# Reordering the seven products of a down projection, with fewer weight loads and the residual loaded by halves

## The chip, the cores and the metric

One core of one Trainium2 chip runs the whole kernel. The metric is device time in microseconds (us). The matmul engine is called PE below, the vector engine DVE, the scalar engine ACT, GpSimd POOL, and the queue that issues most transfers SP.

## The reference

The program is one decoder block on 1024 tokens of width 1024, with 16 meta tokens put ahead of them, all in float32. The part that matters here is the feed-forward layer, which is computed twice, before and after the token mixing:

```python
def _swiglu(x, w_gu, w_down):
    gate, up = jnp.split(x @ w_gu, 2, axis=-1)
    return (jax.nn.silu(gate) * up) @ w_down

h = h + 0.5 * _swiglu(_rmsnorm(h, ffn1_norm[l]), ffn1_w_gu[l], ffn1_w_down[l])
u = _rmsnorm(h, mix_norm[l])
...                                    # mixing: gated delta rule and RWKV-7, added to h
h = h + 0.5 * _swiglu(_rmsnorm(h, ffn2_norm[l]), ffn2_w_gu[l], ffn2_w_down[l])
return _rmsnorm(h, final_norm)[:, N_META:]
```

The hidden width is 2816. The first feed-forward layer works on 1040 columns (tokens and meta tokens), the second on 1024.

## The kernel before

Activations lie transposed, with channels on the 128 partitions and tokens along the free axis. Every float32 matrix product is made of three float32r matmuls: both operands are split into a high part (a copy on ACT into float32r, line 164) and a low part (the difference, on DVE, line 165), and high x high, high x low and low x high are added up in PSUM.

Each feed-forward product is a Strassen-Winograd product over 2 x 2 blocks, so it takes seven block products in place of eight. For the down projection (function `down`, matmuls at line 700) the left blocks are the weights W00, W01, W10, W11 (rows are halves of the 1024 outputs, columns are halves of the 2816 hidden channels), or sums of them. The right blocks are seven *forms* of the hidden activations (`FORMS`): the plain blocks b11, b21, b22, and the differences t1 to t4. Tokens are halved too: n is 520 columns in the first layer and 512 in the second. `ADDS` says to which of the four quadrants of the residual h each product is added (line 706; 0 and 1 are the two token halves of the upper 512 outputs, 2 and 3 those of the lower).

One form is one *round*, called r0 to r6 below in the order of `FORMS`. A round has four output tiles m (`HK` = 4) of 128 rows, and each has 11 blocks of 128 hidden channels, in two weight chunks of 6 and 5 (`CHUNKS`). With three matmuls per block that makes 132 matmuls of 512 columns per round in the second layer, and 264 of 256 or 264 columns in the first, where a row of 520 does not go through one matmul.

The work around each round:

- *Weights.* `weight_order` lists all chunks in the order of their use. `fetchw` loads the next one into a buffer `wraw` (two buffers) from SP's queue, and `down_weights` makes of it what the round needs. In the rounds on sums, POOL adds or subtracts it into a tile `wsum`, which holds one sum per chunk and lasts from round to round. Then the chunk, or its sum, is split into a weight tile (two tiles `w` and a third one, `w3`). `loadw` keeps the fetches two chunks ahead of the one in use.
- *Forms.* The gate and up phase stores its finished forms to device memory (line 530, SP's queue). `Hidden.load` brings those of the next round back in the course of a round (line 670, ACT's queue), and `Hidden.split` splits them in place. `Hidden.arrange` gives the places; while one round reads one set of 11, the other set is loaded.
- *Residual.* In r0 the loop loads the rows of h for output tiles m and m + 4 ahead of tile m's matmuls (lines 780 and 883, SP's queue).
- *The last two rounds of the first layer* go by columns: `down_rounds` yields r5 and r6 for the columns from 256, and then both again for the first 256, so that the norm that follows can start on the later columns. Their weights are fetched twice. Squares for the norm (line 326), the store of h (line 813), and, in the second pass, the normalised input of the mixing (line 825, split at lines 164 and 165) are put behind each output tile by `after`.
- In the second layer, `after` runs the final norm of the second token half behind r4, and that of the first half at the end.

The order of r0 to r6 is b11, t1, t2, b22, t3, b21, t4. The weights they need are W00; W10 + W11; W10 + W11 - W00; W01 less that; W00 - W10; W01; W11. An entry into `wsum` that is not a sum of the last content and one block starts from two loads: r1 loads W10 and W11, r4 loads W00 and W10.

The program is traced in this order, and a planner orders the instructions on each engine's queue by its own estimate of when they are ready; `issue_after` puts an instruction behind a given one on its queue. Each queue is executed in its order.

Of the kernel before, what the change touches and what calls it, by code (L numbers as in the profile page):

```python
# [8 lines left out]
F32 = mybir.dt.float32  # L9
# [36 lines left out]
FORMS = ("b11", "t1", "t2", "b22", "t3", "b21", "t4")  # L46
ADDS = ((0, 1, 2, 3), (1, 3), (1, 2, 3), (1,), (2, 3), (0,), (2,))
NSLOT = 28
LAST = len(FORMS) - 2
# [146 lines left out]
def down_rounds(by_columns):  # L196

    for r in range(LAST):
        yield r, None
    for cols in ((256, T // 2 - 256), (0, 256)) if by_columns else (None,):  # L200
        for r in range(LAST, len(FORMS)):
            yield r, cols


def weight_order():

    def down_order(n):
        for r, _ in down_rounds(n == 1):
            for m in range(HK):
                for k0, kk in CHUNKS:  # L210
                    yield f"wdn{n}", (r, m, k0), kk

    def tiles(cts, j=0):
        for ct in cts:
            yield "win", (ct + j % NJ,), KD

    yield from down_order(1)
    for act, it in schedule():
        yield from tiles(USES.get(act, ()), 0 if act == "segment" else it)
    for _ in range(2):  # L220
        for m in range(KD):
            yield "wout", (m,), KD

    yield None
    yield from down_order(2)


def down_weights(g, name, raw, r, m, k0, kk):

    blk = lambda i, j: g.a[name][m + HK * i][:, HF * j + k0 : HF * j + k0 + kk]  # L230
    dma = g.nc.sync.dma_start
    sums = g.nc.gpsimd.tensor_tensor
    g.wdma = dma(raw, blk(*((0, 0), (1, 1), (0, 0), (0, 1), (1, 0), (0, 1), (1, 1))[r]))
    if r in (0, LAST, LAST + 1):
        return raw
    s = g.wsum[:, m, k0 : k0 + kk]

    def other(i, j):
        with g.tc.issue_after(g.wdma.ins):
            dma(s, blk(i, j))  # L240

    if r == 1:
        other(1, 0)
        sums(s, s, raw, op=ALU.add)
    elif r == 2:
        sums(s, s, raw, op=ALU.subtract)
    elif r == 3:
        sums(s, raw, s, op=ALU.subtract)
    else:
        other(0, 0)  # L250
        sums(s, s, raw, op=ALU.subtract)
# [3 lines left out]
def fetchw(g):  # L255
# [4 lines left out]
    raw = g.wp.tile([P, KD, P], F32, name="wraw", tag="wraw", bufs=2)[:, :kk]  # L260
    if name.startswith("wdn"):
        src = down_weights(g, name, raw, *idx, kk)
    else:
        src = raw
        g.nc.sync.dma_start(raw, g.a[name][idx])
    third = False
    if name.startswith("wdn"):
        g.wcount += 1
        third = g.wcount % 3 == 0
    if third:  # L270
# [7 lines left out]
def loadw(g, name, *idx):  # L278

    while g.wfetched < len(g.worder) and g.worder[g.wfetched]:  # L280
        if g.wfetched > g.wused + AHEAD + g.worder[g.wfetched][0].startswith("wdn"):
            break
# [204 lines left out]
def gate_up(g, which, n, w, b):  # L487
# [93 lines left out]
    for i, (p, gu) in enumerate(units):  # L581
# [34 lines left out]
        else:  # L616
            mul(c21, g21, p, "b21")
            sub(g21, c21, g22, p, "t4")
# [5 lines left out]
class Hidden:  # L624
# [14 lines left out]
    def ahead(self):  # L639
        self.g.wcount = 0  # L640
# [16 lines left out]
        self.split(HF)  # L657
        yield

    def arrange(self, spare, last):  # L660
        e, o = self.even, self.odd
        self.slots = e[:HF] + (o[:HF] + e[:HF]) * 2 + o[HF:] + [spare] + o[:HF] + last

    def load(self, upto, done):
        while len(self.loads) < min(upto, len(self.slots)):
# [4 lines left out]
            self.g.nc.scalar.dma_start(t[:, 1, :].bitcast(F32), self.g.frm[rp][:, : self.n])  # L670
            self.loads.append((rp, t))

    def split(self, upto):
        while len(self.at) < min(upto, len(self.order)):
# [9 lines left out]
def down(g, hs, which, n, hidden, hooks):  # L684

    nc = g.nc
    for r, cols in down_rounds(which == 1):
        for m in range(HK):
            hidden.step(r, m)
            if r == 0:  # L690
                hooks.residual(m)
            pd = mm_tile(g, "pd", n)
            parts = [cols] if cols else halves(n)
            for k0, kk in CHUNKS:
                wd = loadw(g, f"wdn{which}", r, m, k0)
                for c0, cn in parts:
                    for k in range(k0, k0 + kk):
                        x = hidden.at[r, k]
                        for i, (u, v) in enumerate(((0, 0), (0, 1), (1, 0))):
                            nc.tensor.matmul(pd[:, c0 : c0 + cn], lhsT=wd[:, u, k - k0, :], rhs=x[:, v, c0 : c0 + cn],  # L700
                                             start=k + i == 0, stop=k == HF - 1 and i == 2)
            c0, cn = cols or (0, n)
            for o in ADDS[r]:
                t0 = o % 2 * n + c0
                hv = hs[m + o // 2 * HK][:, t0 : t0 + cn]
                nc.vector.scalar_tensor_tensor(hv, pd[:, c0 : c0 + cn], 0.5, hv, op0=ALU.mult, op1=ALU.add)
            hooks.after(r, cols, m)
# [19 lines left out]
def ffn1(g):  # L727
    tc, nc = g.tc, g.nc
    n = T // 2
    with ExitStack() as ctx:  # L730
# [38 lines left out]
        hs = {k: sp.tile([P, T], F32, name=f"h{k}") for k in (3, 7, 2, 0, 4, 1, 5, 6)}  # L769
        sum_tile = lambda shape, dtype: sp.tile(shape, dtype, name="wsum", tag="wsum", bufs=1)  # L770
        g.wsum = sum_tile([P, HK, HF, P], F32)
        spare = sp.tile([P, 2, ROW(n)], F32R, name="form")[:, :, :n]
# [4 lines left out]
        def residual(m):  # L777
            for k in (m, m + HK):
                with tc.issue_after(g.wdma.ins):
                    nc.sync.dma_start(hs[k], g.a["hT"][k])  # L780

        hooks.residual = residual

        def before_last():
            early.close()
            t = sum_tile([P, 5, 2, ROW(n)], F32R)
            hidden.slots += [t[:, i, :, :n] for i in range(5)]
            g.upctx = ExitStack()
# [12 lines left out]
            hooks.todo = []  # L801

        def after(r, cols, m):
# [4 lines left out]
            s = 0 if cols[0] else 1  # L808
            k = m + HK * (r - LAST)
            t0, sn, _ = SEGS[s]  # L810
            rms = hooks.rms[s]
            rms.add(hs[k][:, t0 : t0 + sn])
            nc.sync.dma_start(g.hdr[s][k], hs[k][:, t0 : t0 + sn])
            if k == KD - 1:
                rs = g.un.tile([P, 528], F32, name="nrs", tag="nrs", bufs=2)
                rms.finish(rs)
# [3 lines left out]
                else:  # L820
                    nc.sync.dma_start(g.rdr, rs[:, :sn])
            if s == 1:
                k, rs = hooks.todo.pop(0)
                t = g.un.tile([P, 528], F32, name="nt", tag="nt", bufs=2)
                nc.vector.scalar_tensor_tensor(t, hs[k][:, SEGS[0][0] :], g.V("gm", k), rs, op0=ALU.mult, op1=ALU.mult)
                g.u.append(u_tile(g, t))

# [5 lines left out]
def ffn2(g):  # L833
# [3 lines left out]
    with ExitStack() as ctx:  # L837
# [34 lines left out]
        hs = {k: sp.tile([P, SEQ], F32, name=f"hh{k}") for k in (3, 7, 2, 0, 4, 1, 5, 6)}  # L872
        g.wsum = sp.tile([P, HK, HF, P], F32, name="wsum", tag="wsum", bufs=1)
        hidden.odd = hidden.places("t3", "22", "t4", "t1")
        e = hidden.even
        hidden.arrange(e[HF], e[4:9])
        hooks = K()

        def residual(m):
            for k in (m, m + HK):  # L880
                for s, h in enumerate((g.h2dr, g.h3dr)):
                    with tc.issue_after(g.wdma.ins):
                        nc.sync.dma_start(hs[k][:, s * n : (s + 1) * n], h[k])

        hooks.residual = residual

        def final_tiles(s):
# [6 lines left out]
            hooks.rs, hooks.rows = rows[3], rows[4:]  # L894
# [3 lines left out]
        def after(r, cols, m):  # L898
            s, k = int(r < LAST), m + HK * (r - LAST)
            blk = lambda k: hs[k][:, s * n : (s + 1) * n]  # L900
            if k < 0 and k + 1:
                return
            if s or k == 0:
                hooks.sum = final_tiles(s)
            for i in range(KD - 1) if s else [k] * (k < KD - 1):
                hooks.sum.add(blk(i))
            if not s and k < KD - 1:
                return
            rs = hooks.rs
            hooks.sum.finish(rs, blk(KD - 1))  # L910
            for k in range(KD):
                o = hooks.rows[k % len(hooks.rows)]
# [949 lines left out]
```

## Time and profile before

| | |
|---|---|
| median of 3 runs | 3060.49 us (3057.82 to 3062.16) |
| profiled execution | 3060.95 us, of which 3058.4 us are the span of the trace |
| mean granted TensorE clock | 0.986 |
| PE busy | 2909.5 us, 95% of the span |
| DVE, ACT, POOL busy | 2181.6, 1448.8, 481.8 us |
| r0 to r6 of the first layer | 474.1 to 742.0 us |
| mixing | from 742 us to the second layer |
| r0 to r6 of the second layer | 2805.1 to 3044 us |

A busy PE in the table counts a matmul as busy until its modelled end, and the ends of pipelined matmuls overlap, so the number of matmuls in a stretch says more on its pace than the busy time. The stretches of the rounds are found by counting the matmuls of line 700.

### The profile page before, as it was taken

How to read it: one execution, taken by the hardware profiler on the slowest of the kernel's cores; microseconds unless marked ns; L12 is line 12 of the kernel's file. 1: busy time of each engine (PE TensorE's matmuls, PEld its weight loads, DVE VectorE, ACT ScalarE, POOL GpSimd, SP SyncE). 2: the span in 40 equal slices, each digit the busy share in tenths (PEclk: the TensorE clock that was granted, in tenths of full speed). 3: DMA queues.
4: the chain of work that ended last, by engine and by line, in shares of the span. 5: the costliest groups of instructions: out<-in, count | busy, mean ns of one | idle time of the engine just before them, and what ended most of it. 6: DMA issues, size and time to landing. Idle time of an engine off the chain costs nothing.

```text
span 3058.4 us, 62929 instructions
## 1 busy us (share of the span) xinstructions
PE 2909.5 (95%) x25630; PEld 2510.0 (82%) x25630; DVE 2181.6 (71%) x4103; ACT 1448.8 (47%) x2562; POOL 481.8 (16%) x550
## 2 busy tenths in 40 slices
PE   8999999998999999999998999999999999999898
PEld 8999999997877888888776777777777788887676
DVE  6566667756668777788877887777866766667774
ACT  5222233334646556565566556655644432223343
POOL 0333221512000000000000100000000033331520
PEclk9999999999999999999999999999999999999999
DMA  3233338665222323333232332233354233336753
GB/s 121 94 105 105 105 122 290 193 193 157 84 69 69 76 69 75 77 86 83 86 96 71 79 82 76 77 83 85 103 150 164 77 104 104 104 104 235 240 185 119
DMA packets 295489, 351.51 MB, mean 115 GB/s; under 512 B 173392, under 2 KB 179536, under 8 KB 295200
## 3 DMA queue, kind: packets, MB, share of 16 engines
q1 hardware_dynamic: 271216, 303.44, 33.1%
q10 hardware_dynamic: 23904, 43.86, 4.4%
q8 instruction: 201, 3.29, 0.5%
q14 instruction: 88, 0.72, 0.1%
q0 software_dynamic: 80, 0.19, 0.0%
HBM read 279.50 MB, written 67.91 MB: 114 GB/s over the span
## 4 chain that ended last, share of the span: by engine, by line
PE 48%; DVE 10%; ACT 6%; DMA 3%; issue 2%; POOL 1%; SPq 0%; ACTq 0%; DVEq 0%; POOLq 0%
PE pp L313 16%; PE pg L500 12%; PE pd L700 3%; PE pwo L313 3%; DVE w L165 2%; ACT w L164 1%; PE pg L524 1%; DVE tb L1524 1%; DVE Xb L1526 1%; PE cs L1156 1%; PE vp L1209 1%; DMA wsum<-in_wdn 1%; PE mp L1209 1%; DMA wraw<-in_wdn 1%; DVE mt L1632 1%
## 5 line engine op out<-in xcount | busy, mean ns | idle before, releaser
L313 PE MATMUL pp<-uk,w 128*128 128x512 f32 (+2 forms) x4824 | 967.7, 346 | 13.0 <-DVE w L165 8.1
L313 PEld LDWEIGHTS pp<-uk,w 128*128 128x128 f32 x4824 | 741.5, 190 | 110.2 <-DVE w L165 15.8
L700 PE MATMUL pd<-form,w 128*128 128x256 f32 (+2 forms) x2652 | 444.7, 328 | 43.4 <-DVE w L165 22.3
L165 DVE TENSOR_TENSOR w<-wraw,w 128x1024 fp32r<-128x1024 f32 (+2 forms) x314 | 390.5, 1245 | 122.0 <-ACT w L164 118.8
L700 PEld LDWEIGHTS pd<-form,w 128*128 128x128 f32 x2652 | 393.3, 194 | 93.9 <-DVE w L165 32.3
L164 ACT ACTIVATE w<-wraw 128x1024 fp32r<-128x1024 f32 (+2 forms) x314 | 314.5, 1002 | 269.4 <-PE pg L500 119.7
L500 PE MATMUL pg<-bt,w 128*128 128x256 f32 (+2 forms) x2520 | 400.8, 317 | 0.3 <-DVE w L165 0.3
L500 PEld LDWEIGHTS pg<-bt,w 128*128 128x128 f32 x2520 | 360.2, 188 | 33.4 <-DVE w L165 0.7
L506 DVE TENSOR_TENSOR c<-c,pg 128x520 f32<-128x520 f32 (+1 forms) x280 | 189.3, 688 | 233.0 <-PE pg L500 208.6
L500 PE MATMUL pg<-b,w 128*128 128x256 f32 (+2 forms) x2160 | 347.8, 317 | 0.0
L500 PEld LDWEIGHTS pg<-b,w 128*128 128x128 f32 x2160 | 309.8, 188 | 28.0
L164 ACT ACTIVATE w<-wrx 128x1024 fp32r<-128x1024 f32 (+1 forms) x64 | 58.3, 912 | 282.1 <-PE pg L500 239.6
L470 POOL TENSOR_TENSOR wrx<-wrx 128x512 f32<-128x512 f32 x38 | 52.5, 1383 | 726.0 <-DVE w22b L165 547.8
L164 ACT ACTIVATE w<-wsum 128x768 fp32r<-128x768 f32 x64 | 50.3, 788 | 173.7 <-PE pd L700 58.9
L1526 DVE TENSOR_TENSOR Xb<-Xb,tb 115x126 f32<-115x126 f32 (+22 forms) x496 | 125.1, 252 | 8.8
L1524 DVE TENSOR_TENSOR tb<-Ub,Xb 115x126 f32<-115x126 f32 (+22 forms) x496 | 123.7, 249 | 9.3 <-DMA Ub<-scr 2.2
L1333 DVE SCALAR_TENSOR_TENSOR acc<-xr,pk,acc 128x528 f32<-128x528 f32 (+1 forms) x144 | 108.8, 756 | 28.9 <-ACT acc L1329 28.3
L165 DVE TENSOR_TENSOR form<-form 128x512 fp32r<-128x512 f32 (+1 forms) x149 | 123.1, 871 | 7.5 <-ACT form L164 7.5
L165 DVE TENSOR_TENSOR w<-wsum,w 128x768 fp32r<-128x768 f32 x64 | 75.6, 1187 | 64.3 <-ACT w L164 64.3
L164 ACT ACTIVATE form<-form 128x512 fp32r<-128x512 f32 (+1 forms) x149 | 84.6, 623 | 42.5 <-DMA form<-frm 31.6
L313 PE MATMUL pwo<-uk,w 128*128 128x512 f32 x384 | 99.3, 411 | 4.1 <-DVE w L165 1.9
L313 PEld LDWEIGHTS pwo<-uk,w 128*128 128x128 f32 x384 | 73.4, 196 | 21.6 <-ACT w L164 2.3
(426 smaller groups left out, 4438.6 us busy)
## 6 DMA issues: line engine op xcount, KB each, us to landing
wraw<-in_win SPq DMA_DIRECT2D x150, 512.0 KB
wraw<-in_wdn SPq DMA_DIRECT2D x64, 384.0 KB
wraw<-in_wgu SPq DMA_DIRECT2D x44, 512.0 KB
wrx<-in_wgu SPq DMA_DIRECT2D x44, 512.0 KB
wraw<-in_wdn SPq DMA_DIRECT2D x64, 320.0 KB
frm<-c SPq DMA_DIRECT2D x77, 260.0 KB
frm<-c SPq DMA_DIRECT2D x77, 256.0 KB
form<-frm ACTq DMA_DIRECT2D x77, 256.0 KB
```

The lines of the kernel that those rows point to most:

```text
L164: g.nc.scalar.activation(hi, src, AF.Copy)
L165: (eng or g.nc.vector).tensor_tensor(lo, src, hi.bitcast(F32), op=ALU.subtract)
L313: g.nc.tensor.matmul(ps, lhsT=l, rhs=r, start=i == 0, stop=i == n - 1)
L470: sums.tensor_tensor(a22, a21, a22, op=ALU.add)
L500: nc.tensor.matmul(ps[:, c0 : c0 + cn], lhsT=l[:, x, k, :], rhs=r[:, k, y, c0 : c0 + cn], start=i == 0, stop=i == 3 * HK - 1)
L506: nc.vector.tensor_tensor(o, x, y, op=ALU.add)
L524: nc.tensor.matmul(ps[:, c0 : c0 + cn], lhsT=l[:, x, k, :], rhs=r[:, k, y, c0 : c0 + cn], start=i == 0, stop=i == 6 * HK - 1)
L700: nc.tensor.matmul(pd[:, c0 : c0 + cn], lhsT=wd[:, u, k - k0, :], rhs=x[:, v, c0 : c0 + cn], start=k + i == 0, stop=k == HF - 1 and i == 2)
L1209: g.nc.tensor.matmul(ps[e][HS[dst], c0 : c0 + CB], lhsT=l, rhs=r, start=True, stop=True)
L1333: nc.vector.scalar_tensor_tensor(acc[:, :n], xr[:, tap : tap + n], V("convw", ct * 4 + tap), acc[:, :n], op0=ALU.mult, op1=ALU.add)
L1524: nc.vector.tensor_tensor(tv, U[:, i, i + 1 :].unsqueeze(2).to_broadcast([npt, nt, ncc]), X[:, i, 0:ncc].unsqueeze(1).to_broadcast([npt, n ...
L1526: nc.vector.tensor_tensor(X[:, i + 1 :, 0:ncc], X[:, i + 1 :, 0:ncc], tv, op=ALU.add)
```

## The change

- `FORMS` becomes t4, t1, t2, b22, b11, t3, b21, so the weights of r0 to r6 are W11; W10 + W11; W10 + W11 - W00; W01 less that; W00; W00 - W10; W01. From one to the next sum only one block is new. In r0 and in r4 a block is loaded straight into `wsum` and split from there, without `wraw` (tile 0 of r0 is still loaded through `wraw`, and again into `wsum` for r1). The number of chunk loads goes from 88 to 58 in the first layer and from 72 to 58 in the second. POOL still has 32 sums per layer.
- `ADDS` follows. t4 goes to one quadrant, so r0 needs only the first token half of the lower rows. The residual is loaded by token halves: 12 of 16 halves in the course of r0, and the first halves of the upper rows in r3, before b11 adds to all four quadrants in r4.
- The form of block 10 of t4, the last result of the gate and up phase, is not stored and loaded but split directly (`Hidden.direct`).
- Only the last round, b21, goes by columns in the first layer. Its eight weight chunks are kept for the second pass: six of them in the places of the forms t3 and 22, which are free once r5 has ended. In the second pass the first two weights of the mixing are fetched, after its output tiles 0 and 1. Their fetch within `loadw` is held off until then.
- b21 adds to the upper rows alone, so the squares and the stores of the lower rows (tiles 4 to 7, both token segments) are put between r5 and r6, and in the second pass two tiles of the mixing's input follow each output tile instead of one.
- In the second layer the final norm of the second token half stands behind r5, with the first squares of the other half.
- `wsum` is placed ahead of five of the residual's eight tiles in memory.

```diff
-FORMS = ("b11", "t1", "t2", "b22", "t3", "b21", "t4")
-ADDS = ((0, 1, 2, 3), (1, 3), (1, 2, 3), (1,), (2, 3), (0,), (2,))
-LAST = len(FORMS) - 2
+FORMS = ("t4", "t1", "t2", "b22", "b11", "t3", "b21")
+ADDS = ((2,), (1, 3), (1, 2, 3), (1,), (0, 1, 2, 3), (2, 3), (0,))
+LAST = len(FORMS) - 1
...
 def down_weights(g, name, raw, r, m, k0, kk):
     blk = lambda i, j: g.a[name][m + HK * i][:, HF * j + k0 : HF * j + k0 + kk]
+    def dma(t, i, j):
+        with ExitStack() as behind:
+            if g.wdma and t is not raw:
+                behind.enter_context(g.tc.issue_after(g.wdma.ins))
+            ins = g.nc.sync.dma_start(t, blk(i, j))
+        if t is raw:
+            g.wdma = ins
+
+    if r == LAST or (r == 0 and m == 0):
+        dma(raw, *((0, 1) if r else (1, 1)))
         return raw
     s = g.wsum[:, m, k0 : k0 + kk]
+    if r in (0, 4):
+        dma(s, r == 0, r == 0)
+        return s
+    if r == 1 and m == 0:
+        dma(s, 1, 1)
+    dma(raw, *((1, 0), (0, 0), (0, 1), None, (1, 0))[r - 1])
+    x, y = (raw, s) if r == 3 else (s, raw)
+    g.nc.gpsimd.tensor_tensor(s, x, y, op=ALU.add if r == 1 else ALU.subtract)
     return s
...
+    if down and idx[0] == LAST and g.held:
+        w = g.held.pop(0)
+    elif down and g.wcount % 3 == 0:
         w = g.wthird.tile([P, 2, CHUNKS[0][1], P], F32R, name="w3", tag="w3", bufs=1)
...
+            if p < HF - 1:
+                sub(g21, c21, g22, p, "t4")
+            else:
+                nc.vector.tensor_tensor(g21, c21, g22, op=ALU.subtract)
+                g.direct(g21)
...
+    def direct(self, src):
+        rp, t = self.loads[HF - 1]
+        split(self.g, src, t[:, 0, :], t[:, 1, :])
+        self.at[rp] = t
...
+    for r in range(len(FORMS)):
+        cols = halves(n)
+        kept = {}
         for m in range(HK):
             hidden.step(r, m)
+            hooks.before(r, m)
+
+            def w(k0):
+                kept[m, k0] = loadw(g, f"wdn{which}", r, m, k0)
+                return kept[m, k0]
+
+            product(r, m, (w, w), cols[-1:] if r == LAST else cols)
+            hooks.after(r, m, 0)
+        if r == LAST and len(cols) > 1:
+            for m in range(HK):
+                w = lambda k0: kept[m, k0]
+                product(r, m, (w, w), cols[:1])
+                if m < 2:
+                    fetchw(g)
+                hooks.after(r, m, 1)
+
+
+def residuals(r, m, load):
+
+    if r == 0:
+        if m == 0:
+            load(HK, 0)
+        if m + 1 < HK:
+            load(HK + m + 1, 0)
+        load(m, 1)
+        load(m + HK, 1)
+    if r == 3:
+        load(m, 0)
...
         def before_last():
             early.close()
             t = sum_tile([P, 5, 2, ROW(n)], F32R)
             hidden.slots += [t[:, i, :, :n] for i in range(5)]
+            hidden.load(len(hidden.slots), LAST)
+            for x in ("t3", "22"):
+                t = pools[x].tile([P, 3, 2, CHUNKS[0][1], P], F32R, name="w", tag=f"b{x}", bufs=1)
+                g.held += [t[:, i] for i in range(3)]
...
+            for s in range(2):
+                for k in range(HK, KD):
+                    squares(s, k)
```

177 lines of the change are left out of this document (79 added, 98 removed).

## The prediction, made before the change was run

> **What bounds the kernel now.** I read the page's first part (busy times), then counted the matmuls of line 700 to find the seven rounds of each layer, and then asked each round for its waits, its transfers and its engines in order of time.
>
> ```profile
> span 3058.4 us, 62929 instructions
> PE 2909.5 (95%) x25630; PEld 2510.0 (82%) x25630; DVE 2181.6 (71%) x4103; ACT 1448.8 (47%) x2562; POOL 481.8 (16%) x550
> ```
>
> PE is the bound of the whole, so only stretches in which it starves can give time. The stretches of r0 to r4 of the first layer, and of r5 with r6 in two column passes, with line 700 alone (stretch, length, PE busy and matmuls, weight loads, granted clock, DMA share, GB/s):
>
> ```profile
> 474.10:513.20 39.10, 34.20 (x264) 33.72 (x265) 0.91 0.93 328
> 513.20:550.20 37.00, 33.87 (x266) 33.28 (x265) 0.95 0.74 245
> 550.20:589.90 39.70, 35.20 (x266) 34.49 (x265) 0.91 0.60 183
> 589.90:621.40 31.50, 31.50 (x266) 31.50 (x265) 1.00 0.65 221
> 621.40:655.10 33.70, 32.24 (x267) 31.80 (x266) 1.00 0.58 177
> 655.10:697.90 42.80, 38.14 (x288) 35.19 (x287) 1.00 0.68 189
> 697.90:742.00 44.10, 35.16 (x243) 32.86 (x243) 0.92 0.60 172
> ```
>
> The fourth row is a round without a gap: 266 matmuls in 31.5 us, 0.1184 us each, so 264 need 31.3 us. Against that the rows lose 7.8, 5.7, 8.4, 0.2 and 2.4 us, and the two column passes, 528 matmuls or 62.5 us in 86.9 us, lose 24.4: 48.9 us in all. The second layer, r0 to r6:
>
> ```profile
> 2805.10:2839.90 34.80, 31.24 (x132) 24.33 (x132) 1.00 1.01 363
> 2839.90:2881.10 41.20, 33.55 (x128) 25.89 (x129) 0.92 0.75 243
> 2881.10:2914.90 33.80, 31.94 (x132) 25.46 (x131) 0.95 0.60 188
> 2914.90:2946.20 31.30, 31.30 (x139) 25.91 (x138) 1.00 0.70 235
> 2946.20:2980.40 34.20, 31.02 (x134) 24.58 (x133) 1.00 0.45 143
> 2980.40:3013.60 33.20, 30.76 (x134) 24.66 (x133) 1.00 0.53 170
> 3013.60:3044.00 30.40, 30.01 (x133) 24.52 (x131) 1.00 0.20 56
> ```
>
> Here 139 matmuls take 31.3 us, so 132 need 29.7; the losses are 5.1, 11.5, 4.1, 1.6, 4.5, 3.5 and 0.7, together 31.0 us. Both layers lose 79.9 us, and that is all the change can win in them.
>
> Why they lose it. In r0 the DMA engines are full: the transfers from 470 to 512 us are
>
> ```profile
> DMA packets 5932, 13.93 MB, mean 332 GB/s; under 512 B 671, under 2 KB 671, under 8 KB 5928
> ...
> form<-frm ACTq DMA_DIRECT2D x17, 260.0 KB
> h<-in_hT SPq DMA_DIRECT2D x8, 520.0 KB
> frm<-c SPq DMA_DIRECT2D x6, 260.0 KB
> ...
> wsum<-in_wdn SPq DMA_DIRECT2D x2, 384.0 KB
> wsum<-in_wdn SPq DMA_DIRECT2D x1, 320.0 KB
> ```
>
> and a weight chunk behind the residual comes late. In r1 and r2 ACT's splits wait for the sums, which begin from two loads in r1 (474 to 590 us; waits in total, times, longest):
>
> ```profile
> ACT w L164 <- POOL wsum L244: 15.2, 5, 6.5
> ACT w L164 <- POOL wsum L248: 12.3, 1, 12.3
> ```
>
> The second row names r3's first sum (line 248) while PE wants a chunk of r2: a split stood behind form loads on ACT's queue, and these behind SP's loads ahead. PE's timeline shows the gap of r0, and the pace of a column pass (start, length, matmuls, idle before):
>
> ```profile
> 502.67 0.79 PE L700 MATMUL pd<-form,w 128*128 128x256 f32 x2 [4.68 <-ACT w L164]
> ...
> 678.66 2.20 PE L700 MATMUL pd<-form,w 128*128 128x264 f32 x16 [0.48 <-DVE w L165]
> ...
> 684.26 2.20 PE L700 MATMUL pd<-form,w 128*128 128x264 f32 x16 [0.48 <-DVE w L165]
> ```
>
> An output tile of a column pass takes 684.26 - 678.66 = 5.6 us where 33 matmuls need 3.9: weights bound it. SP's queue shows why (655 to 742 us): the raw loads, for two buffers, queue behind the store of h, which waits for its last addition.
>
> ```profile
> SPq L233 <- DVE h L706: 27.8, 12, 3.1
> ```
>
> **The change part by part.** The sum is made against the profiled execution, 3060.95 us (span 3058.4), 0.46 above the median of 3060.49.
>
> *r0.* Of the 13.93 MB go four halves of 266 KB of the residual (1.07 MB, moved to r3), the store and the load of one form (0.53) and the early `wsum` loads for r1 (1.1): 11.2 MB, at 332 GB/s 33.8 us in place of 42. That is still longer than 31.3, and part of it lies ahead of 474 us. I take a loss of 2.5 us instead of 7.8 (between 0.2, r3's row, and the present 7.8), in the second layer 2 instead of 5.1. In r3 the added 1.07 MB raise 221 GB/s to about 255, well below 328, and cost nothing while the form loads stay on time; uncovered they are 3.2 us at 332.
>
> *The direct form.* Its subtraction is the last row here (DVE in order of time):
>
> ```profile
> 477.44 0.69 DVE L533 TENSOR_TENSOR c<-c,c 128x520 f32<-128x520 f32 x1
> ```
>
> A split behind it (0.64 on ACT, 0.70 on DVE, rows below) ends near 479.6 us. PE begins r0 at 474.1 and wants block 10 after 48 matmuls, 5.7 us later, at 479.8. Cover is just enough; I take 0, and up to 1 us if DVE's other forms go first. The residual's first tile now lies at the far end of its pool; DVE, on which the weights' low parts queue, would wait for it. I price that within r0's bounds.
>
> *r1 and r4.* r1 loses 8 of its 16 chunk loads (7, since tile 0's two come back and one of r0's three was early), r4 its eight sums and eight of its 16 loads, and all use of `wraw`. r4 takes over all four additions; r0 loses 12 on DVE. r1: 2.5 us lost instead of 5.7 and 4 instead of 11.5 (lower end 0.2, upper end the present rows). r4: 1 instead of 2.4 and of 4.5.
>
> *r2 and r3.* Same loads and sums as now; what they gain is that r1 hands over without arrears. But ACT's queue can still stand behind SP's. I take 5 instead of 8.4 and 1 instead of 0.2 in the first layer (the residual's halves are new there), 3 instead of 4.1 and 1.5 instead of 1.6 in the second; ends are r3's row and the present ones.
>
> *r5 and r6 of the first layer.* Now r5 runs over all columns on sums with one load each: 31.3 + 2 us, as r4's row. r6 is two passes of 132 matmuls, 15.6 us each. Sixteen chunk fetches go, with their splits. Rows of the work around, first layer, by shape (busy, mean ns):
>
> ```profile
> L165 DVE TENSOR_TENSOR uk<-nt,uk 128x528 fp32r<-128x528 f32 x8 | 7.8, 979 | 0.0
> L825 DVE SCALAR_TENSOR_TENSOR nt<-h,pk,nrs 128x528 f32<-128x528 f32 x8 | 7.0, 891 | 0.1
> L326 ACT ACTIVATE nsq<-h 128x528 f32<-128x528 f32 x8 | 5.1, 635 | 4.0 <-DVE h L706 4.0
> L165 DVE TENSOR_TENSOR wsum<-wsum 128x520 fp32r<-128x520 f32 x5 | 3.4, 698 | 0.2 <-ACT wsum L164 0.2
> L164 ACT ACTIVATE wsum<-wsum 128x520 fp32r<-128x520 f32 x5 | 3.2, 637 | 0.7 <-DMA wsum<-frm 0.6
> ```
>
> Pass one is still bound by weights. Two chunks are ready, which carry 3.9 us of tile 0; tiles 1 to 3 at 5.6 us make 20.7. On the border, five forms that come late into `wsum`'s place (3.2 us on ACT) and eight squares (5.1) share ACT with the next splits, eight stores share SP, and the kept weights wait until r5 has released t3 and 22. Ready work may pass most of it; I add 4 (between 0 and the 8.3 of both rows): 24.7. Pass two needs no weights: 15.6 + 1.5. So r5 and r6 take 33.3 + 24.7 + 17.1 = 75.1 instead of 86.9, 11.8 less. The eight inputs of the mixing, 8 x (0.979 + 0.891) = 15.0 us of DVE, now have one pass as cover and end some 3 us after it; but PE meets the eighth only after 48 matmuls. The present handover:
>
> ```profile
> 742.00:748.30 6.30, 2.53 (x9) 1.52 (x10) 5.64 (x5) 2.63 (x3) 4.72 (x8) 0.88 0.44 149
> ```
>
> PE does 9 matmuls in 6.3 us, for want of the mixing's first weights. These are now fetched in pass two; late next is the last input. I take 2 us less (ends: 4 less, 3 more).
>
> *r5 and r6 of the second layer.* r5: 2 lost instead of 3.5. The final norm of one half moves from ahead of r5 to ahead of r6, with four more squares on ACT (2.5 us at 0.635): 4.5 instead of 0.7. The tail behind the last matmul is the same: 0.
>
> *Sum.* First layer: 5.3 + 3.2 + 3.4 - 0.8 + 1.4 + 11.8 + 2.0 = 26.3. Second: 3.1 + 7.5 + 1.1 + 0.1 + 3.5 + 1.5 - 3.8 = 13.0. Together 39.3 us: 3060.95 - 39.3 = 3021.6, for the median too.
>
> A gap costs more than its length. The ten microseconds around the gap of 4.68 us ran at two thirds of the clock, though matmuls filled the second half of them (engines PE to POOL, then clock and DMA):
>
> ```profile
> 500.00:510.00 10.00, 7.13 (x39) 6.84 (x40) 5.34 (x8) 2.38 (x4) 1.83 (x1) 0.66 0.81 288
> ```
>
> My losses per round hold that already, since they are read from whole rounds. The Trainium skill, "TensorE: Matmul & The Clock Gate", section "HAM oscillation — how this bites in real kernels", says that idle gaps of more than about 3.4 us set the array to half its clock, and it is slow again at the start of the next stretch. By that rule the row agrees. It speaks against the border of r5 and r6: by that page my 4 us there, in one gap, would bring half of another 3.4 us, 1.7 us by estimate, and the sum would be 3023.3, which is inside the forecast's case.
>
> **The rivals.**
>
> *Most is hidden or comes back.* If arrears in r0 to r3 come from queues and not from volume, these rounds keep their losses, and only r4 to r6 and the handover gain: 1.4 + 11.8 + 2.0 and 3.5 + 1.5 - 3.8, 16.4 us: 3044.6. For it speaks the wait of 12.3 us, in a round with one load per chunk, as all are after the change; against it r3, equally built, at full clock.
>
> *All full rounds run as r3.* Then r0 to r5 of the first layer lose 0.2 each, and all seven of the second 1.6, with the column passes and the handover as forecast. That is 2.3 + 2.3 + 4.8 + 0.8 + 0.8 + 1.8 = 12.8 us more from the first layer and 18 - 11.2 = 6.8 more from the second: 3002.0. For it speaks that every loss up to r2 follows the full DMA engines of r0; against it, that r3 is one row of thirteen.
>
> *Slower.* SP and POOL run ahead on sums with one load each, since a sum frees `wraw` and not PE; form loads stand behind them, and splits behind those. If every round on sums (r1, r2, r3, r5) stalls like today's worst, 8.4 us in the first layer and 11.5 in the second, they cost 4 x 8.4 + 4 x 11.5 = 79.6 in place of the 21 I charge: 3080.2. It decides from (21 + 39.3) / 8 = 7.5 us per such round; today's eight (r1 to r4) average 38.4 / 8 = 4.8. For it speaks the same wait of 12.3 us; against it, that these loads get fewer and r3 has none of it.
>
> **How the numbers follow.** Forecast 0.58, hidden 0.17, all as r3 0.12, slower 0.08, and 0.05 for a mixture that ends within 0.2% (6 us, about what a measurement of this kernel tells from no change). Faster: 0.58 + 0.17 + 0.12 = 0.87. The range from 3002 to 3050 holds the forecast, most of the hidden case and half of the r3 case, 0.8.
>
> **What would show it.** DMA below 300 GB/s in r0, and no gap of 4 us there; r1 near 34 us in both layers and line 244 not waiting for `wsum` loads; r4 without POOL; 58 chunk loads per layer; pass one near 25 us with its gaps at the border, pass two near 17 without; the first projection of the mixing soon behind it. Wrong would be gaps in front of r2's chunks with form loads standing on ACT's queue, or DVE waiting for the residual in r0, or more than 8 us at either layer's last border.

## The result and the profile after

| | before | changed |
|---|---|---|
| median | 3059.15 us (3057.15 to 3062.16, 4 runs) | 3026.98 us (3025.39 to 3030.14, 4 runs) |
| profiled execution | 3060.95 us, span 3058.4 | 3030.14 us, span 3028.2 |
| r0 to r6, first layer | 267.9 us | 242.6 us |
| r0 to r6, second layer | 238.9 us | 230.9 us |

The ratio is 0.9895, with a 95% interval of 0.9878 to 0.9912: 32.2 us faster, where 39.3 were forecast. In the spans it is 30.2 us. The first part of the page of the changed kernel:

```profile
span 3028.2 us, 62795 instructions
PE 2895.7 (96%) x25630; PEld 2505.8 (83%) x25630; DVE 2165.3 (72%) x4083; ACT 1438.0 (47%) x2546; POOL 480.2 (16%) x550
```

The stretches of r0 to r6 of the first layer, matmuls of line 700 alone (stretch, length, PE, weight loads, clock, DMA share, GB/s):

```profile
474.70:516.80 42.10, 34.36 (x265) 33.45 (x265) 0.92 0.86 301
516.80:558.00 41.20, 35.74 (x267) 35.00 (x267) 0.92 0.62 188
558.00:589.50 31.50, 31.50 (x266) 31.50 (x265) 1.00 0.65 211
589.50:621.00 31.50, 31.50 (x266) 31.50 (x265) 1.00 0.63 202
621.00:652.60 31.60, 31.60 (x266) 31.60 (x266) 1.00 0.48 144
652.60:684.30 31.70, 31.70 (x267) 31.70 (x266) 1.00 0.39 131
684.30:717.30 33.00, 32.04 (x264) 31.53 (x262) 1.00 0.58 177
```

Rounds r2 to r5 have no gap left, and the column round r6 loses 1.7 us. The rest of the loss is in the first two rows, and these are *longer* than before (39.1 and 37.0). In the second layer r0 is longer too (34.8 before), r1 is shorter (41.2 before), and both still lose most:

```profile
2781.80:2822.00 40.20, 33.15 (x133) 26.45 (x134) 0.87 0.89 312
2822.00:2858.80 36.80, 32.40 (x134) 25.65 (x133) 0.95 0.63 198
2858.80:2891.40 32.60, 30.60 (x134) 24.52 (x133) 1.00 0.68 211
...
2981.20:3012.70 31.50, 30.31 (x133) 24.55 (x131) 1.00 0.36 121
```

PE's timeline has the gap of r0, right behind tile 0 (start, length, matmuls, idle before), in the first layer and then in the second:

```profile
481.33 0.38 PE L700 MATMUL pd<-form,w 128*128 128x256 f32 x1 [0.84 <-ACT form L163]
482.15 2.31 PE L700 MATMUL pd<-form,w 128*128 128x256 f32 x17 [0.44 <-DVE form L164]
490.74 0.80 PE L700 MATMUL pd<-form,w 128*128 128x256 f32 x2 [6.27 <-ACT w L163]
...
2796.52 3.92 PE L700 MATMUL pd<-form,w 128*128 128x512 f32 x8 [7.01 <-ACT w L163]
```

SP's queue says why the split of tile 1's first chunk is late:

```profile
478.26 4.84 SPq L815 DMA_DIRECT2D h<-in_hT  x4
483.69 2.19 SPq L226 DMA_DIRECT2D wsum<-in_wdn  x2
```

Tile 1 goes straight into `wsum`, whose memory is free only when gate and up have ended, and its load stands behind four residual halves. In the kernel before, three chunks were loaded through `wraw` and split ahead of r0; now two are. Call this theory *place and queue*; the rival is the prediction's own, *volume*. In r1 ACT's queue shows a block of form loads, and a split behind it:

```profile
513.47 11.69 ACTq L674 DMA_DIRECT2D form<-frm  x4
525.28 0.84 ACT L163 ACTIVATE w<-wsum 128x768 fp32r<-128x768 f32 x1 [11.13 <-PE pd L700]
```

From the first to the last, four issues took 11.69 us where a single one takes 0.34. The row puts the split's wait down to PE, but what stood ahead of it on ACT were these issues.

### The profile page after: what moved, and what is told of

It is laid out like the page before. It is cut to its first block, busy times and chain, and to the rows that moved or that the text cites. A ratio compares the mean times of both kernels' runs of the same rounds, so it can differ in the third digit from the quotient of the medians.

```text
span 3028.2 us, 62795 instructions
## 1 busy us (share of the span) xinstructions
PE 2895.7 (96%) x25630; PEld 2505.8 (83%) x25630; DVE 2165.3 (72%) x4083; ACT 1438.0 (47%) x2546; POOL 480.2 (16%) x550
## 2 busy tenths in 40 slices
DMA packets 289727, 334.57 MB, mean 110 GB/s; under 512 B 172752, under 2 KB 178896, under 8 KB 289440
## 3 DMA queue, kind: packets, MB, share of 16 engines
q1 hardware_dynamic: 265744, 287.05, 31.8%
## 4 chain that ended last, share of the span: by engine, by line
PE 46%; DVE 12%; ACT 5%; DMA 3%; issue 2%; POOL 1%; SPq 1%; DVEq 0%; ACTq 0%; POOLq 0%
PE pp L306 14%; PE pg L493 12%; PE pd L700 4%; PE pwo L306 3%; DVE w L164 2%; DVE tb L1575 1%; PE pg L517 1%; DVE Xb L1577 1%; ACT w L163 1%; DMA wraw<-in_wdn 1%; PE cs L1207 1%; PE vp L1260 1%; PE mp L1260 1%; DVE mt L1683 1%; PE np L1260 1%
## 5 line engine op out<-in xcount | busy, mean ns | idle before, releaser
L700 PE MATMUL pd<-form,w 128*128 128x256 f32 (+2 forms) x2652 | 432.0, 325 | 26.6 <-ACT w L163 14.7
L164 DVE TENSOR_TENSOR w<-wraw,w 128x1024 fp32r<-128x1024 f32 (+2 forms) x270 | 352.9, 1307 | 83.5 <-ACT w L163 79.9
L163 ACT ACTIVATE w<-wraw 128x1024 fp32r<-128x1024 f32 (+2 forms) x270 | 279.8, 1036 | 208.0 <-PE pg L493 127.7
L163 ACT ACTIVATE w<-wsum 128x768 fp32r<-128x768 f32 x92 | 72.7, 791 | 228.1 <-PE pd L700 145.7
L164 DVE TENSOR_TENSOR w<-wsum,w 128x768 fp32r<-128x768 f32 x92 | 95.9, 1048 | 85.7 <-ACT w L163 85.7
L241 POOL TENSOR_TENSOR wsum<-wsum,wraw 128x768 f32<-128x768 f32 (+1 forms) x48 | 93.2, 1955 | 229.1 <-DMA wsum<-in_wdn 106.6
L163 ACT ACTIVATE form<-form 128x512 fp32r<-128x512 f32 (+1 forms) x147 | 83.0, 622 | 27.6 <-DMA form<-frm 11.6
```

The lines of the kernel that those rows point to most:

```text
L163: g.nc.scalar.activation(hi, src, AF.Copy)
L164: (eng or g.nc.vector).tensor_tensor(lo, src, hi.bitcast(F32), op=ALU.subtract)
L241: g.nc.gpsimd.tensor_tensor(s, x, y, op=ALU.add if r == 1 else ALU.subtract)
```

## The experiments

Each kernel is the changed one with one edit, unless said otherwise. Times are medians; ratios are to the kernel before in the same set of runs.

**The changed kernel again.** 

> The changed kernel itself once more, beside the experiments of the same chip, so that their rows have a row to stand against. Expected 3025 to 3030 us, a gap of 6 to 7 us behind tile 0 of r0 in both layers (the first: 66 matmuls, then 6.3 us; the second: 33 matmuls, then 7.0), r0 of 42 and 40 us. If the gap belongs to one execution's chance, it is not there again.

Measured: 3030.31 us, ratio 0.9902 (0.9887 to 0.9917), with gaps of 5.87 and 6.62 us at the same places. This is the bar for the next three.

**Tile 1 of r0 through wraw** (r1 then loads W11 again for two tiles).

```diff
-    if r == LAST or (r == 0 and m == 0):
+    if r == LAST or (r == 0 and m < 2):
-    if r == 1 and m == 0:
+    if r == 1 and m < 2:
```

> Tile 1 of r0 takes its two weight chunks through wraw as tile 0 does, and r1 loads W11 for tile 1 into wsum again: two loads more per layer. Theory Q (queue and place): the gap behind tile 0 comes because the first chunk that goes to wsum cannot be fetched while the gate and up phase holds the memory, and then stands behind four residual halves on SP's queue, while wraw could be filled ahead. Then the gap goes: PE runs 132 matmuls (66 in the second layer) without it, r0 falls from 42.2 and 40.3 us to 33 to 37, the whole by 6 to 13 us, to about 3017. A smaller wait may come up at tile 2. Rival V (volume): r0 moves 301 to 312 GB/s and is late because of the bytes; two loads more make it no better: 3027, or 1 to 3 us slower.

Measured: 3021.69 us, 0.9878 (0.9861 to 0.9894), 8.6 us below the changed kernel with two loads more per layer. The gap is now behind tile 1 in both layers, and smaller:

```profile
493.76 0.67 PE L700 MATMUL pd<-form,w 128*128 128x256 f32 x2 [3.20 <-ACT w L163]
...
2796.38 37.11 PE L700 MATMUL pd<-form,w 128*128 128x512 f32 x152 [4.11 <-ACT w L163]
```

More bytes and a shorter time: volume does not set r0. But r0 of the first layer still takes 38.7 us, where 33 to 37 were expected (36.8 in the second), and what was won in r1 (33.6 and 30.8 us) is mostly lost again in r2, which takes 38.8 and 38.3 us instead of 31.5 and 32.6.

**Residual behind each tile's weights.** `hooks.before(r, m)` is called in `product`, after the weights of the tile, instead of ahead of it.

> The residual's loads of each tile are issued behind that tile's weight fetches instead of ahead of them; same loads, same bytes. Theory Q: the first wsum chunk is issued at the end of the gate and up phase, some 4 to 5 us earlier (the four residual halves took SP from 478.3 to 483.1 us), and lands as much earlier; the gap of 6.3 us falls to 1 to 3 in both layers, the half clock behind it goes, the whole falls by 6 to 12 us, to about 3018. DVE may wait for the residual of tile 0 (its loads come 2 us later), which costs PE nothing while three output banks are free. Rival V: bytes alone count, r0 stays at 40 to 42 us, 3027. Rival R: the residual becomes late, DVE stands before it and the weights' low parts behind: slower by 3 to 10 us.

Measured: 3024.21 us, 0.9885 (0.9869 to 0.99), 6.1 us below, though the intervals of the two overlap. The gap behind tile 0 is 2.22 us in the first layer and 4.05 in the second.

**The whole residual in r0** (all 16 halves; none in r3).

> All 16 halves of the residual are loaded in r0 (four per tile), none in r3: this undoes the residual's part of the change, with loads still cut into halves. Forecast's account (volume): 1.07 MB more in r0, 3.2 us at 332 GB/s in the first layer, about as much in the second: r0 longer by 3 us in each, 3033. Theory Q: what counts is how many loads stand ahead of a weight chunk on SP. Four stand ahead of tile 1's chunks either way, so the gap behind tile 0 stays as it is; tiles 2 and 3 get one more each ahead of them, r0 longer by 0 to 2 us: 3027 to 3030. r3 the same.

Measured: 3029.19 us, 0.9902 (0.9886 to 0.9917), the changed kernel's time. Four halves more in r0 cost nothing that shows in the whole (r0 takes 43.4 and 39.5 us), so moving them to r3 saved nothing that shows either.

**Both edits of r0 at once.**

> Tile 1 of r0 comes through wraw, and the residual halves are issued behind each tile's weights, both at once. Theory (r0's gap comes from the place of the first wsum load: its memory is free late and it stands behind residual halves on SP's queue): the first removes the late memory for tile 1, the second the residual ahead of tile 2's loads. They act at different tiles, so the gains of 8.6 us and 6.1 us over the changed kernel (3030.3 us in the same runs) should mostly add: 3016 to 3019 us, and no gap over 2.5 us behind tile 0 or 1 in either layer. Rival 1 (both remove one and the same wait): no more than the first alone, 3020 to 3023 us. Rival 2 (r0 is bound by bytes: over 40 us at full DMA whatever the order): no better than 3024 us, the gap moves to tile 2 with 3 us or more.

Measured: 3016.21 us, 0.9862 (0.9845 to 0.9879). The gains of the two mostly add up: some 12 us by the ratios, where each alone gave 8.6 and 6.1. r0 and r1 of the first layer, then r0 of the second:

```profile
473.00:506.90 33.90, 32.09 (x265) 31.69 (x266) 1.00 0.99 345
506.90:546.00 39.10, 33.80 (x266) 33.35 (x266) 0.96 0.69 211
...
2769.10:2799.50 30.40, 30.31 (x133) 24.82 (x134) 1.00 0.99 361
```

With DMA busy 0.99 of the time r0 loses 2.6 and 0.7 us: full DMA engines do not stall it.

**The new order with the old loading** (r0 and r4 through `wraw`, r1 and r5 from two loads, 72 loads per layer).

> The new order of the forms with the old way of loading: r0 and r4 through wraw, r1 and r5 start their sums from two loads (72 chunk loads in place of 58 per layer). Theory (place and queue, not volume, set r0; single loads pay in r1 and r5 only): r0's gap behind tile 0 shrinks below 3 us, since three chunks are split ahead as in the kernel before; r1 and r5 each lose 2 to 5 us more; the kernel lies between 3024 and 3034 us, within 4 us of the changed one. Rival (bytes and POOL's sums bind r0 and r1): r0 and r1 together are longer than in the changed kernel by 5 us or more per layer, and the kernel is at 3040 us or above.

Measured: 3032.34 us, 0.9917 (0.9903 to 0.9931), not told apart from the changed kernel by the intervals. Rows of r0 to r2 and r5:

```profile
474.30:507.90 33.60, 32.25 (x266) 31.85 (x266) 1.00 0.89 306
507.90:541.50 33.60, 32.12 (x266) 31.66 (x265) 1.00 0.73 258
541.50:588.90 47.40, 35.67 (x267) 33.73 (x266) 0.93 0.67 207
...
652.00:683.60 31.60, 31.60 (x267) 31.60 (x266) 1.00 0.80 252
```

r0's gap went, as the theory said, but r1 with its two loads ran well too, and r2 lost 16 us instead: r0 to r2 take 114.6 us, and 114.8 in the changed kernel (in the second layer 110.5 and 109.6). The theory had r1 and r5 worse by 2 to 5 us; as the queues stand, single loads buy nothing that shows. What stalls r2 is on ACT's queue again:

```profile
541.13 9.54 ACTq L669 DMA_DIRECT2D form<-frm  x3
550.79 0.74 ACT L163 ACTIVATE w<-wsum 128x640 fp32r<-128x640 f32 x1 [13.61 <-DMA wraw<-in_wdn]
```

**Form loads of r1 to r6 from SP's queue.** One line of `Hidden.load`:

```diff
-                self.g.nc.scalar.dma_start(t[:, 1, :]...
+                (self.g.nc.sync if rp[0] else self.g.nc.scalar).dma_start(t[:, 1, :]...
```

> The loads of the forms for r1 to r6 are issued from SP's queue instead of ACT's; everything else is the changed kernel. Theory (the weight splits on ACT stand behind form loads that themselves wait for the raw loads on SP, and these for POOL's sums): ACT's queue no longer shows a block of form loads of 8 to 12 us in r1, the gap in front of r1's second tile goes, r1 is 34 us instead of 37 to 41 in both layers, and the kernel is 4 to 8 us faster than the changed one. The gap behind tile 0 of r0 stays. Rival (the form loads only move the wait: on SP they stand behind the same raw loads and come later): a round waits for its own forms instead, r1 or r2 stays above 37 us, and the kernel is no faster, or slower by up to 10 us.

Measured: 3021.83 us, 0.9867 (0.985 to 0.9884), against 0.9895 and 0.9902 without the edit: some 8 to 11 us. On SP's queue eight form loads are now issued in 4.67 us:

```profile
510.64 4.67 SPq L674 DMA_DIRECT2D form<-frm  x8
```

r1 takes 35.9 and 29.8 us, instead of 41.2 and 36.8 (rows of r1 in the first layer, of r1 and r2 in the second):

```profile
515.50:551.40 35.90, 33.40 (x267) 33.20 (x266) 0.95 0.67 212
...
2815.60:2845.40 29.80, 29.80 (x134) 24.66 (x133) 1.00 0.60 181
2845.40:2882.70 37.30, 32.43 (x134) 25.58 (x133) 0.95 0.71 229
```

A part of the second layer's loss moved on to r2 (32.6 before the edit, 37.3 with it), so the rival has a grain of truth.

**The same line in the kernel before.** Old order, old loads.

> The kernel before, old order and old loads, with one edit: the loads of the forms for r1 to r6 go through SP's queue instead of ACT's. Theory (the losses of r1 and r2 in both kernels come from splits standing behind form loads on ACT, not from the number of weight loads): r1 and r2 of both layers, which lose 14 and 16 us here, lose some 4 us less in each layer, and the kernel is 6 to 12 us faster than before, as the changed kernel gains 8 us by the same edit. Rival (with two weight loads per sum SP's queue is fuller, and in r5 and r6 the form loads stand behind the stores of h): the form loads come late, r4 to r6 lose what r1 and r2 win, and the time is within 4 us of before or longer.

Measured: 3040.07 us, 0.9934 (0.9921 to 0.9948), 20.9 us faster than before, twice what the theory gave. r0 and r1 of the first layer and of the second:

```profile
473.30:505.10 31.80, 31.77 (x265) 31.62 (x265) 1.00 0.90 329
505.10:538.30 33.20, 31.91 (x265) 31.71 (x266) 1.00 0.90 296
...
2795.40:2826.00 30.60, 30.49 (x133) 24.61 (x132) 1.00 0.98 344
2826.00:2857.50 31.50, 30.32 (x133) 24.79 (x134) 1.00 0.91 299
```

r0 fell from 39.1 to 31.8 us, which the theory had not named, and r1 from 37.0 to 33.2 and from 41.2 to 31.5 with two loads for every chunk. A part moved on: r2 of the second layer rose from 33.8 to 38.9 us, and r4 of the first from 33.7 to 36.3. In the trace of before, ACT splits forms as they land and then the weight chunk that PE waits for; the chunk itself landed 0.2 us after the last of these splits, so they did not hold it:

```profile
500.84 0.64 ACT L164 ACTIVATE form<-form 128x520 fp32r<-128x520 f32 x1 [1.28 <-DMA form<-frm]
501.77 1.57 ACT L164 ACTIVATE w<-wraw 128x768 fp32r<-128x768 f32 x2 [0.29 <-DMA wraw<-in_wdn]
```

SP's queue shows why it came late (before, then with the edit):

```profile
484.32 10.31 SPq L780 DMA_DIRECT2D h<-in_hT  x6
494.72 1.61 SPq L233 DMA_DIRECT2D wraw<-in_wdn  x2
...
481.66 2.83 SPq L780 DMA_DIRECT2D h<-in_hT  x6
484.59 3.51 SPq L233 DMA_DIRECT2D wraw<-in_wdn  x2
```

The two chunks of the last tile stood behind six residual loads, whose issue took 10.31 us before and 2.83 with the edit, so they went out some 10 us earlier.

With the forms on SP in both kernels the ratios are 0.9934 and 0.9867: of the change's 32 us some 20 are left. The traces have all of these in r5 and r6 of the first layer, which take 86.6 us here and 65.9 in the changed kernel with the same line; the other rounds come out even, within 2 us per layer.

**All three edits at once** (tile 1 through `wraw`, weights ahead of the residual, forms on SP).

> Tile 1 of r0 through wraw, residual behind the weights, and the form loads on SP's queue: three edits at once. Theory (after the first two, what is left in r1 and r2 is ACT's queue behind form loads): r0 to r2 together fall from 106.7 us (first layer, first two edits alone) to below 100, and the kernel is at 3008 to 3012 us, 4 to 8 us below the first two alone. Rival (POOL's sums and their raw loads, in lockstep over two buffers, set r1 and r2): no gain beyond 2 us over the first two alone (3016 us), the waits in r1 then name POOL's sums or the raw loads.

Measured: 3007.88 us, 0.9824 (0.9803 to 0.9844), the fastest kernel of the study, 54 us below the one before. By the ratios it is some 12 us below both edits of r0 alone. r0 to r2 of the first layer take 102.6 us, not below 100. In the stretch of r1 (all engines: PE, weight loads, DVE, ACT, POOL) DVE is now busy 36.57 of 39 us:

```profile
506.00:545.00 39.00, 35.62 (x281) 35.01 (x279) 36.57 (x31) 15.53 (x24) 26.59 (x14) 0.96 0.74 230
```

With both edits of r0 alone, whose r1 lies in the same stretch, DVE had 32.83 us. What is left in r1 looks like DVE's backlog beside POOL's sums; no run took that apart.

**The last pass fetches its weights again** (the kept ones are not used, and the mixing's first fetches are not held off).

> The first layer's last pass fetches its eight chunks again instead of using the kept ones. Theory (the kept weights are what lifts pass two from 5.6 us per output tile to 3.9): pass two takes 21 to 23 us instead of about 16, the first projection of the mixing waits less, since DVE's inputs have more cover, and the kernel is 2 to 6 us slower than the changed one (3032 to 3036 us where that gives 3030). Rival (pass one, which fetches its weights too and ran without gaps, shows that the fetch is not what bounds a column pass; the old passes were slow for the stores and additions between them): pass two stays under 18 us and the kernel is within 1.5 us of the changed one.

Measured: 3035.14 us, 0.9928 (0.9912 to 0.9945), some 8 us slower than the changed kernel. The two passes of r6 in the changed kernel:

```profile
684.30:700.80 16.50, 16.32 (x133) 16.04 (x132) 1.00 0.66 197
700.80:717.30 16.50, 15.72 (x133) 15.49 (x132) 1.00 0.51 157
```

And with the edit:

```profile
681.00:698.30 17.30, 16.68 (x133) 16.13 (x132) 1.00 0.62 186
698.30:722.80 24.50, 18.62 (x134) 17.46 (x132) 0.93 0.57 170
```

Pass two grows from 16.5 to 24.5 us, more than the 21 to 23 expected. Pass one fetches eight chunks in both kernels and hardly loses anything. By the program, six of its chunks have a place of their own, while a fetch in the other pass needs one of the three weight tiles back from PE; that this is the difference is likely, but no run shows it alone.

**Half of the mixing's inputs on POOL.** The low part of every second `uk` is made by GpSimd.

> The low part of every second mixing input (four of eight) is made on POOL instead of DVE. Theory (the handover of 9.4 us has its gap of 4.4 us because DVE's backlog of inputs puts the last addition of the down projection late): four subtractions of about 0.98 us leave DVE, the gap falls to 1 to 2 us, and the kernel is 2 to 4 us faster than the changed one. Rival (the first projection waits for the input tiles themselves): POOL's subtraction takes two to three times as long as DVE's, the gap stays at 4 us or grows, and the time is the changed kernel's within 2 us or longer.

Measured: 3030.12 us, 0.9911 (0.9897 to 0.9926): no gain. The gap ahead of the first projection is longer, 6.34 us instead of 4.43. Groups of DVE from 700 to 725 us in the changed kernel (busy, mean ns):

```profile
L866 DVE SCALAR_TENSOR_TENSOR nt<-h,pk,nrs 128x528 f32<-128x528 f32 x8 | 6.8, 872 | 0.1
L164 DVE TENSOR_TENSOR uk<-nt,uk 128x528 fp32r<-128x528 f32 x8 | 6.3, 821 | 0.0
```

And with the edit:

```profile
L866 DVE SCALAR_TENSOR_TENSOR nt<-h,pk,nrs 128x528 f32<-128x528 f32 x8 | 8.7, 1123 | 0.1
L164 DVE TENSOR_TENSOR uk<-nt,uk 128x528 fp32r<-128x528 f32 x4 | 4.9, 1225 | 0.0
```

In these groups DVE does four instructions less and is busy 13.6 us instead of 13.1. The means mix two kinds: in both traces an instruction takes 0.7 to 0.8 us, or 1.7 to 1.8 when it begins while a TENSOR_TENSOR of POOL runs. Two of the sixteen did so in the changed kernel, five of the twelve with the edit.

**Inputs of the mixing behind their tile's addition**, on top of both edits of r0.

> Tile 1 of r0 through wraw, residual behind the weights, and in the last pass each input of the mixing behind the addition of its own output tile on DVE. Theory (the handover's gap of 4.4 us is the last addition standing behind two ready inputs on DVE): the last addition starts within 1 us of the last matmul of the pass, PE's gap ahead of the first projection falls to 2 us or less, and the handover is 2 to 3 us shorter, some 2 us below the first two edits alone (3016 us). Rival (DVE is full in pass two, so the order only changes what is late): the gap moves to the inputs of the first projection and the handover stays at 9 us.

Measured: 3016.46 us, 0.9851 (0.9837 to 0.9866), no different from both edits alone (0.9862). PE's gap at the handover in the changed kernel:

```profile
721.93 4.19 PE L306 MATMUL pp<-uk,w 128*128 128x272 f32 x17 [4.43 <-DVE h L707]
```

And its gaps with the edit:

```profile
714.50 2.83 PE L306 MATMUL pp<-uk,w 128*128 128x272 f32 x11 [3.01 <-DVE h L709]
...
721.06 3.17 PE L306 MATMUL pp<-uk,w 128*128 128x272 f32 x24 [1.64 <-DVE bdr L1017]
```

The gap is 1.4 us shorter, and one of 1.64 us comes behind it. The rival holds: from 704 to 718 us DVE is busy 13.87 of 14 us, and order only chooses what is late.

## Why the prediction was right, and where it was not

The direction and most of the size were right, by terms that missed to both sides. That 32.4 us worse and 23.3 better nearly cancel is luck. Losses per term in the profiled execution, by the prediction's own 31.3 and 29.7 us per round:

| term | forecast | measured | difference |
|---|---|---|---|
| r0 and r1, first layer | 5.0 | 20.7 | 15.7 worse |
| r0 and r1, second layer | 6.0 | 17.6 | 11.6 worse |
| r2 to r5, first layer | 9.0 | 1.1 | 7.9 better |
| r2 to r5, second layer | 7.5 | 3.6 | 3.9 better |
| r6, first layer (its length) | 41.8 | 33.0 | 8.8 better |
| r6, second layer | 4.5 | 1.8 | 2.7 better |
| start, mixing with its handover, tail | -2.0 | +3.1 | 5.1 worse |

Together 9.1 us worse: 39.3 - 9.1 = 30.2, the difference of the spans.

*r0.* The step that failed is the first: "11.2 MB, at 332 GB/s 33.8 us". It took the DMA engines for the bound because they were full. The runs show full engines with hardly a loss (31.8 us at 0.90 in the kernel before with its forms on SP, 30.4 at 0.99 in the second layer with both edits of r0), a loss that shrinks when loads are added, and one that stays when the residual's bytes come back. By the first layer's traces r0 lost its time, before and after, to weight chunks that stood behind residual loads on SP's queue; after, also to the place of tile 1's weights. The prediction had this in passing ("a weight chunk behind the residual comes late") but priced bytes, and it left out that `wsum` becomes free later than `wraw`. Its own signs failed there: DMA ran at 301 and 312 GB/s, and gaps of 6.27 and 7.01 us came where none of 4 was to be. It also had tile 0's form at "0, and up to 1": it cost 0.84 + 0.44 us.

*r1.* "Loses 8 of its 16 chunk loads", hence 2.5 and 4 us: the loads did go, and the loss did not. Two loads per chunk run at 33.2 and 31.5 us once the forms are on SP. The mechanism that counts was in the prediction, in "a split stood behind form loads on ACT's queue, and these behind SP's loads ahead", but it was charged to r2 alone. The slower rival built on it had the right cause in the wrong rounds: r3 and r5 do not stall, and r2 loses 0.2 and 2.9 us.

*r2 to r5.* Forecast with arrears; they came through clean but for r2 of the second layer, so here the rival "all full rounds run as r3" was right. r4 without POOL is clean as forecast, but so is r5, which has POOL's sums, even from two loads in the run with the old loading (31.6 us): sums alone do not make a round lose. The prediction also misread r3 of the second layer as losing 1.6 us: its row holds 139 matmuls and no gap, so this came from where the row was cut.

*r6, first layer.* Pass two is right: 17.1 forecast, 16.5 measured, and keeping the weights is worth 8 us by the run without. Pass one was mis-sized, 24.7 against 16.5: its 5.6 us per tile were read off passes with three weight tiles, and most of the kept chunks have places of their own, which would explain it. The 4 us on the border did not come either, and so the clock rule added nothing there. r6 of the second layer had the right sign (0.7 before, 1.8 after) and less than half the size.

*Handover.* Forecast 2 us better, it is worse: with start and tail 3.1 us go the other way, of which the stretch from r6 to the second layer has 1.4 (2063.1 us before, 2064.5 after). That DVE ends some 3 us late was forecast; that PE meets it only after 48 matmuls was wrong, since its first projection waits for the last addition of r6, which stands among the inputs on DVE. Over the profiles of all these kernels that stretch took between 2060.8 and 2069.1 us, so the size stays open.

*Volume.* DMA moved 334.57 MB instead of 351.51, and no run shows that this was worth anything in time. What the change did win lies in r2 to r6, and 22.2 us of it in r5 and r6 of the first layer (86.9 us before, 64.7 after): one round less by columns and a last pass without fetches. Of these the run without the kept weights isolates some 8; no run takes the rest apart.

*Why a load waits at its issue.* The traces show it by their semaphores. The transfers of SP and ACT all tell of their landing on eight semaphores, which both queues share, and a load can stand until the one that used its semaphore before has landed. Of the four issues of 11.69 us the second went out at 519.37 us, 0.02 us behind the landing of a weight chunk that SP had issued at 515.18; the fourth at 524.84, just behind the landing of another (524.76) and a signal of PE's (524.82). Each of these chunks had waited for a sum of POOL's. In r0 of the kernel before, two of the six residual loads stood in the same way behind an earlier one of the six; with the forms on SP each of the six had a semaphore of its own. No run changed the semaphores alone, so what this is worth stays open.

## What to carry to other kernels

A full DMA row is no proof that the round is bound by bytes: look at which load the engine waits for, and what stands ahead of that load on its queue. Do not issue loads that can wait from an engine on whose computing the bound depends; moving one issue line was worth 21 us here, two thirds of the whole reordering. When weights get a new place, ask from when on that place is free, not only how many loads it saves.

## What the runs showed of the hardware

A DMA issue is not always cheap for the engine that issues it: 11.69 us for four on ACT, with a weight split behind them. The Trainium skill, "DMA: Bandwidth & Descriptors", section "Issuing engines are not separate DMA queues", says that initiating transfers on several engines saves only the time to initiate them, "usually small relative to the DMA itself"; its section "Anatomy of one DMA — SWDGE (gpsimd) path" says that a wait on a semaphore happens on the issuing sequencer before dispatch. The second sentence is what the trace shows on ACT's queue (519.37 us, above), and the first does not cover it: the same loads on the other queue gave 8 to 11 us in one kernel and 20.9 in the other.

DVE gets slower beside POOL: an instruction on 128x528 takes 0.7 to 0.8 us, and 1.7 to 1.8 when it begins while POOL adds or subtracts. Beside POOL's MEMSET it stays at 0.69 and 0.77. The Trainium skill, "SBUF — State Buffer", section "Who interferes with whom", says that a DVE instruction with two inputs in SBUF contends with a GpSimd instruction that reads SBUF, and not with one that only writes it; these times agree. Five slow instructions instead of two cost DVE about the 2.8 us that the four subtractions had taken it.

A gap still costs more than its length: in r0 of the first layer PE waited 0.84 + 0.44 + 6.27 = 7.55 us and the round lost 10.8, at a mean clock of 0.92. Short gaps do it too, against the prediction's rule of about 3.4 us: in r1 of that layer none is longer than 2.47 us and the mean clock is 0.92 as well; with all three edits at once the longest in r1 is 1.81 us, and the clock 0.95.
